# A load of 24 KB to each of 16 partitions, put in the middle of a max-pooling kernel as 15 rows and one row

## The chip, the cores and the metric

One core of one Trainium2 chip. The metric is the device time of one execution in microseconds (us). The kernel before takes 335.85 us (median of 3 runs, 335.66 to 336.07). The profiled span is about 1.8 us shorter than the time of the same run.

## The reference

A one-dimensional max pooling. `x` is 32 x 256 x 4096 in float32; each output is the maximum of 16 consecutive inputs:

```python
def reference(x, output_size):            # output_size = 256, length = 4096
    for i in range(output_size):
        start = int(i * length / output_size)
        end = int((i + 1) * length / output_size)
        result[:, :, i] = np.max(x[:, :, start:end], axis=-1)
```

So 134.2 MB are read, 8.4 MB are written, and each input is used once. There are 2,097,152 windows of 16 elements (64 bytes of input, 4 bytes of output).

## The kernel before

The windows are taken as one long row and dealt to 128 partitions in two groups. Input comes through a ring of three slots. Each slot takes 760 windows per partition (48,640 bytes), VectorE reduces the slot into a result tile, and the results are stored at the end. SyncE issues all DMAs in the order of the program.

```python
    SLOTS = 3
    CHUNK = 760
    GROUPS = [10 * CHUNK, total - 10 * CHUNK]     # windows per partition: 7600, 8784
    ring = pool.tile([P, SLOTS, CHUNK * W], fp32, tag="ring", name="ring")
    # ... (result tiles and DRAM views cut)
    for g, n in enumerate(GROUPS):
        # ... (views of the group cut)
        for a in range(0, n, CHUNK):
            b = min(a + CHUNK, n)
            slot = ring[:, n_loads % SLOTS, 0 : (b - a) * W]
            n_loads += 1
            nc.sync.dma_start(out=slot, in_=xg[:, a * W : b * W])
            nc.vector.reduce_max(out=outs[g][:, a:b],
                in_=slot.rearrange("p (n w) -> p n w", w=W), axis=mybir.AxisListType.X)
        # ... (list of stores cut: group 0; group 1 up to column 7600; the rest)
    for dst, src in stores:
        nc.sync.dma_start(out=dst, in_=src)
```

That makes 22 loads, 21 of them full and the last of 424 windows, and 3 stores.

## Time and profile before

| | before |
|---|---|
| time | 335.85 us |
| DMA queue, share of 16 engines' span | 99.1% |
| VectorE busy | 276.3 us of 334.0 |
| one full load lands every | 14.38 us |
| one full reduction takes | 12.82 us |

From the page of the profile of the kernel before: the span, the busy time of VectorE (DVE), the DMA queue with its packets, megabytes and share of 16 engines' time, the chain of work that ended last, and the group of reductions (busy us, mean ns; then the idle time ahead of them and what ended it).

```profile
span 334.0 us, 111 instructions
...
DVE 276.3 (83%) x22; POOL 0.2 (0%) x4
...
q1 hardware_dynamic: 3600, 142.61, 99.1%
...
DMA 68%; DVE 27%; DVEq 2%; SPq 0%; issue 0%
...
L59 DVE TENSOR_REDUCE out<-ring 128x760 f32<-128x12160 f32 (+1 forms) x22 | 276.3, 12565 | 49.2 <-DMA ring<-in_x_dram 49.2
...
```

The DMA engines have no free time. VectorE waits 49.2 us in all, always for a load. That the chain gives VectorE 27% does not make it a limit: a reduction frees the slot that a later load needs, but that load then stands in a queue that is not empty.

The timeline of the kernel before, at the landings of loads 8 to 11 (loads are counted from 0; start us, length us, engine, line, operation, and in brackets how long the engine was idle and what it waited for):

```profile
...
133.06 12.82 DVE L59 TENSOR_REDUCE out<-ring 128x760 f32<-128x12160 f32 x1 [1.56 <-DMA ring<-in_x_dram]
147.43 12.82 DVE L59 TENSOR_REDUCE out<-ring 128x760 f32<-128x12160 f32 x1 [1.56 <-DMA ring<-in_x_dram]
161.81 12.82 DVE L59 TENSOR_REDUCE out<-ring 128x760 f32<-128x12160 f32 x1 [1.56 <-DMA ring<-in_x_dram]
176.20 12.82 DVE L59 TENSOR_REDUCE out<-ring 128x760 f32<-128x12160 f32 x1 [1.57 <-DMA ring<-in_x_dram]
...
```

Each reduction begins 14.38 us after the one before it, at the moment when its load has landed, after 1.56 us of idling. These starts are therefore the landing times of the loads. From the table of DMA issues (count, KB each, median us from issue to landing), of before:

```profile
...
ring<-in_x_dram SPq DMA_DIRECT2D x21, 6080.0 KB, 30.3
out_dram<-out SPq DMA_DIRECT2D x2, 3800.0 KB, 30.1
...
```

30.3 us is two periods: a load is issued while the load ahead of it still has all of its 14.4 us to go and the one ahead of that its last 1.5 us. The DMA engines thus hold about 16 us of work whenever a new load is issued.

And from the table of stretches of before (columns: from:to, length, busy us and count of VectorE and GpSimd, TensorE clock, mean share of the DMA engines, GB/s):

```profile
...
133.00:147.40 14.40, 12.82 (x1) 0.00 (x0) 1.00 1.00 432
147.40:161.80 14.40, 12.82 (x1) 0.00 (x0) 1.00 1.00 432
...
```

### The profile page before, as it was taken

The page shows a single profiled execution, that of the slowest core. Times are in us where ns is not written, and L with a number is a line of the kernel's source. Part 1 is how long each engine was busy: PE and PEld are TensorE (multiplying, and loading weights), DVE is VectorE, ACT ScalarE, POOL GpSimd, SP SyncE. Part 2 cuts the span into 40 slices and gives each one's busy share as a digit, 9 for nine tenths or more (in the row PEclk, how much of TensorE's full clock was granted, in tenths as well). Part 3 has the DMA queues.
Part 4 walks back from the last instruction along what each step waited for, and adds up shares of the span by engine and source line. Part 5 has one row for each costly group of instructions (what it writes and reads, how often), then busy time and mean ns, then how long its engine had stood idle before and what let it go on. Part 6 is the DMA issues. An engine that isn't in the chain of part 4 may idle for free.

```text
span 334.0 us, 111 instructions
## 1 busy us (share of the span) xinstructions
DVE 276.3 (83%) x22; POOL 0.2 (0%) x4
## 2 busy tenths in 40 slices
DVE  0088989889898988989898898988989898898990
POOL 0000000000000000000000000000000000000000
DMA  9999899999999999999998999999999999989997
GB/s 361 390 460 454 384 466 437 402 466 437 402 460 425 419 454 408 443 454 396 454 454 384 466 437 402 466 419 419 460 414 431 454 408 443 454 384 440 443 419 306
DMA packets 3600, 142.61 MB, mean 427 GB/s; under 512 B 400, under 2 KB 400, under 8 KB 528
## 3 DMA queue, kind: packets, MB, share of 16 engines
q1 hardware_dynamic: 3600, 142.61, 99.1%
HBM read 134.22 MB, written 8.39 MB: 427 GB/s over the span
## 4 chain that ended last, share of the span: by engine, by line
DMA 68%; DVE 27%; DVEq 2%; SPq 0%; issue 0%
DMA ring<-in_x_dram 68%; DVE out L59 27%; DVEq L102 2%; SPq L58 0%
## 5 line engine op out<-in xcount | busy, mean ns | idle before, releaser
L59 DVE TENSOR_REDUCE out<-ring 128x760 f32<-128x12160 f32 (+1 forms) x22 | 276.3, 12565 | 49.2 <-DMA ring<-in_x_dram 49.2
L88 POOL MEMSET const-bfloat16-1.0<- 128x1 bf16 x1 | 0.1, 101 | 0.0
L88 POOL MEMSET const-uint8-127<- 128x1 uint8 x1 | 0.1, 101 | 0.0
L88 POOL MEMSET const-float32-0.0<- 128x1 f32 x1 | 0.1, 98 | 0.2 <-issue 0.2
L88 POOL MEMSET const-float32-1.0<- 128x1 f32 x1 | 0.1, 98 | 0.0
## 6 DMA issues: line engine op xcount, KB each, us to landing
ring<-in_x_dram SPq DMA_DIRECT2D x21, 6080.0 KB, 30.3
out_dram<-out SPq DMA_DIRECT2D x2, 3800.0 KB, 30.1
ring<-in_x_dram SPq DMA_DIRECT2D x1, 3392.0 KB, 23.9
out_dram<-out SPq DMA_DIRECT2D x1, 592.0 KB, 7.6
```

What stands on the lines that cost most here:

```text
L59: nc.vector.reduce_max(out=outs[g][:, a:b], in_=slot.rearrange("p (n w) -> p n w", w=W), axis=mybir.AxisListType.X,)
L88: nc = _bacc.Bacc("TRN2", target_bir_lowering=False, num_devices=1)
L102: with _tile.TileContext(nc) as tc:
```

## The change

One load more is placed after the eleventh load. It takes 384 windows (24,576 bytes) to each of partitions 0 to 15, 393 KB in all, and passes through the ring like any other load. It is issued as two DMAs. The intention was that the one for 15 rows runs on 15 of the 16 DMA engines, and that all 16 share the last row, which is written as 16 pieces. One DMA engine would then carry about 23 KB less than the others (24,576 less 1,536 bytes): an attempt at levelling the engines. The last full-width load shrinks from 424 to 376 windows, so all bytes are still moved exactly once.

```diff
-    total = B * C * O // P
+    total = B * C * O
+    SIDE_P, SIDE, SIDE_AT = 16, 384, 11
+    rest = (total - SIDE_P * SIDE) // P
+    GROUPS = [10 * CHUNK, rest - 10 * CHUNK]
 ... (helpers cut: group(), next_slot(), pooled(), load() do what the loop did)
+    xs, os_ = group(SIDE_P, SIDE)
+    side_out = pool.tile([SIDE_P, SIDE], fp32, tag="side", name="side")
+    def load_side():
+        slot = next_slot(SIDE_P, SIDE)
+        last = SIDE_P - 1
+        nc.sync.dma_start(out=slot[0:last], in_=xs[0:last])
+        nc.sync.dma_start(
+            out=slot[last:SIDE_P].rearrange("p (k n) -> p k n", k=16),
+            in_=xs[last:SIDE_P].rearrange("p (k n) -> p k n", k=16),
+        )
+        pooled(side_out, slot)
 ...
         for a in range(0, n, CHUNK):
+            if n_loads == SIDE_AT:
+                load_side()
+            load(o, xg, a, min(a + CHUNK, n))
 ...
+    stores.insert(1, (os_, side_out))
```

More of the change, by code (lines that the diff above doesn't have):

```diff
@@ L28 @@
     W = L // O
-    total = B * C * O // P
+    total = B * C * O
     SLOTS = 3
     CHUNK = 760
-    GROUPS = [10 * CHUNK, total - 10 * CHUNK]
+    SIDE_P, SIDE, SIDE_AT = 16, 384, 11
+    rest = (total - SIDE_P * SIDE) // P
+    GROUPS = [10 * CHUNK, rest - 10 * CHUNK]
     CUT = 10 * CHUNK
-    assert sum(GROUPS) == total and B * C * O % P == 0
     pool = ctx.enter_context(tc.tile_pool(name="pool", bufs=1))
     ring = pool.tile([P, SLOTS, CHUNK * W], fp32, tag="ring", name="ring")
-    outs = [
-        pool.tile([P, n], fp32, tag=f"out{i}", name=f"out{i}")
-        for i, n in enumerate(GROUPS)
-    ]
@@ L44, with group, next_slot @@
     xw = x.flatten_outer_dims().rearrange("r (o w) -> (r o) w", w=W)
     ow = out.flatten_outer_dims().rearrange("r o -> (r o)")
+    taken = 0
+    def group(parts, n):
+        nonlocal taken
+        span = slice(taken, taken + parts * n)
+        taken += parts * n
+        return (
+            xw[span].rearrange("(p n) w -> p (n w)", p=parts),
+            ow[span].rearrange("(p n) -> p n", p=parts),
+        )
+    n_loads = 0
+    def next_slot(parts, n):
+        nonlocal n_loads
+        slot = ring[0:parts, n_loads % SLOTS, 0 : n * W]
+        n_loads += 1
+        return slot
@@ new lines, in pooled, with load @@
+    def pooled(dst, src):
+        nc.vector.reduce_max(
+            out=dst,
+            in_=src.rearrange("p (n w) -> p n w", w=W),
+            axis=mybir.AxisListType.X,
+        )
+    def load(dst, src, a, b):
+        slot = next_slot(P, b - a)
+        nc.sync.dma_start(out=slot, in_=src[:, a * W : b * W])
+        pooled(dst[:, a:b], slot)
+    xs, os_ = group(SIDE_P, SIDE)
[7 more added lines that the diff above has]
+            in_=xs[last:SIDE_P].rearrange("p (k n) -> p k n", k=16),
+        )
+        pooled(side_out, slot)
@@ L47 @@
     stores = []
-    n_loads = 0
-    first = 0
     for g, n in enumerate(GROUPS):
-        xg = xw[first : first + P * n].rearrange("(p n) w -> p (n w)", p=P)
-        og = ow[first : first + P * n].rearrange("(p n) -> p n", p=P)
-        first += P * n
+        xg, og = group(P, n)
+        o = pool.tile([P, n], fp32, tag=f"out{g}", name=f"out{g}")
         for a in range(0, n, CHUNK):
-            b = min(a + CHUNK, n)
-            slot = ring[:, n_loads % SLOTS, 0 : (b - a) * W]
-            n_loads += 1
-            nc.sync.dma_start(out=slot, in_=xg[:, a * W : b * W])
-            nc.vector.reduce_max(
-                out=outs[g][:, a:b],
-                in_=slot.rearrange("p (n w) -> p n w", w=W),
-                axis=mybir.AxisListType.X,
-            )
-        if g < len(GROUPS) - 1:
-            stores.append((og, outs[g]))
-        else:
-            for a, b in ((0, CUT), (CUT, n)):
-                stores.append((og[:, a:b], outs[g][:, a:b]))
+            if n_loads == SIDE_AT:
+                load_side()
+            load(o, xg, a, min(a + CHUNK, n))
@@ L70 @@
+        for a, b in ((0, CUT), (CUT, n)):
+            if a < b:
+                stores.append((og[:, a:b], o[:, a:b]))
+    assert taken == total
+    stores.insert(1, (os_, side_out))
     for dst, src in stores:
```

## The prediction

> **What bounds the kernel now.** The DMA engines: the queue table gives 99.1% of 16 engines' span. VectorE is busy 276.3 of 334.0 us. In the timeline a full load (128 x 12160) lands every 14.38 us and its reduction takes 12.82 us, so VectorE waits 1.56 us per load. The chain of waits names VectorE (27%) only because a reduction frees a load's slot; that load then still queues behind a whole other one (median 30.3 us from issue to landing, two periods). What matters is bytes per DMA engine, gaps between packets, and which engine finishes last.
>
> In the trace each load has 16 completion arrivals, always spread by 0.92 to 0.96 us: two engines trail (the last 0.13 us behind the second, 0.43 us behind the third). The spread is there at the first load and does not grow: a start offset, not a slow engine.
>
> **What the change does.** Total bytes are the same. The last load shrinks from 6784 to 6016 columns; the 393 KB move into the side load. The order of issues shows one 15x6144 and one 1x6144 DMA after eleven loads, a 16x384 reduction, and one more store.
> [...]
> A 48,640-byte packet takes 1.793 us, 27.1 GB/s per engine.[...] Levelling both laggards could give at most 0.43 us.
>
> **The new hazard.** The side load takes a ring slot for under 1 us of DMA, so the load after it is issued only 1.55 us before the load ahead of the side load lands. The queue then holds about 2.5 us of work, against 16 us normally. At the start, first packets appear 1.0 to 1.4 us after issue (one engine 2.4), and data flows at full rate 1.6 to 2.6 us after it. That nearly fits: I expect one bubble of 0 to 0.4 us[...].
> The side reduction, 6144 elements per partition, costs about 6.5 us of VectorE (from 12.82 us for 12160 and 7.21 for 6784). VectorE falls about 4 us behind and regains 1.56 us per load; the ring's slack hides it. The last reduction is 0.8 us shorter, but the stores queue behind DMA, so no gain.
>
> **Predicted: 336.05 us, from 335.5 to 336.7.** Faster by over 2%: 0.005; within 2%: 0.985; slower by over 2%: 0.01.
>
> **What shows each step.** Queue share still about 99%; full loads 14.38 us apart except one interval of about 15.5 us; VectorE busy about 282 us with a 16-partition reduction near 6.5 us; two or three reductions after it start without waiting; gaps between an engine's packets only just after the side load; the spread of arrivals changed after it.
>
> **What would make it wrong.** The 15-row or one-row DMA on few engines (up to +1 us); [...]a larger bubble (+1 to +3 us); trailing engines really slowed by something the lighter engine relieves (-0.4 us); a different chip's DMA rate.

Where the text shows a cut, passages are taken out that say how the two DMAs are dealt to the DMA engines, which no run had shown, and with them the terms of the sum and two remarks that hang on them. The sum came to about +0.2 us: 0.06 us for the 1.5 KB more assumed on each of 15 engines (at 27.1 GB/s), and three more DMAs at about 0.04 us each, an estimate from the trace of before (14.38 us less 8 packets of 1.793). With 335.85 us before the change that gives 336.05. That the last engine would be spared 23 KB (about 0.8 us) was not expected to shorten the time.

## The result, and the profile after

| | before | after |
|---|---|---|
| time, median (range) | 335.86 us (335.66 to 336.07, 6 runs) | 340.04 us (339.33 to 340.85, 6 runs) |
| span of the profiled run | 334.0 us | 338.5 us |
| DMA queue, share | 99.1% | 98.7% |
| VectorE busy | 276.3 us | 281.9 us |

The ratio is 1.0124 (95% interval 1.0109 to 1.0139): the change makes the kernel 4.2 us slower. Ratios and intervals here and below are from runs of the same rounds, so not quite the ratio of the medians quoted. The loss is within the 2% band, but well above the predicted range.

The page of the changed kernel, the same lines:

```profile
span 338.5 us, 117 instructions
...
DVE 281.9 (83%) x23; POOL 0.2 (0%) x4
...
q1 hardware_dynamic: 3664, 142.61, 98.7%
...
DMA 63%; DVE 30%; issue 3%; DVEq 2%; SPq 0%
...
L67 DVE TENSOR_REDUCE out<-ring 128x760 f32<-128x12160 f32 (+1 forms) x22 | 275.5, 12528 | 48.1 <-DMA ring<-in_x_dram 48.1
L67 DVE TENSOR_REDUCE side<-ring 16x384 f32<-16x6144 f32 x1 | 6.5, 6529 | 0.0
...
```

The DMA share hardly moved, and this is the trap. A packet counts as busy from its start to its end, however slowly it gets on: here packets of 24,576 bytes took up to 3.23 us, where a full load's pace gives 0.91 (below), and all of it is in the share. What the engines moved shows the loss. The table of stretches of the changed kernel:

```profile
...
132.90:147.26 14.36, 12.82 (x1) 0.00 (x0) 1.00 1.00 434
147.26:163.27 16.01, 12.82 (x1) 0.00 (x0) 1.00 1.06 388
163.27:182.00 18.73, 18.71 (x2) 0.00 (x0) 1.00 0.94 393
...
```

The stretch in which load 10 lands is 16.01 us instead of 14.40. The DMA share is there 1.06, over 1 because a packet counts whole in the stretch in which it starts, and the packets that start last in it run long; and yet the rate falls from 434 to 388 GB/s. The timeline of the changed kernel shows where:

```profile
...
132.91 12.82 DVE L67 TENSOR_REDUCE out<-ring 128x760 f32<-128x12160 f32 x1 [1.57 <-DMA ring<-in_x_dram]
145.75 0.40 SPq L84 DMA_DIRECT2D ring<-in_x_dram  x1
146.21 0.23 SPq L85 DMA_DIRECT2D ring<-in_x_dram  x1
147.28 12.82 DVE L67 TENSOR_REDUCE out<-ring 128x760 f32<-128x12160 f32 x1 [1.56 <-DMA ring<-in_x_dram]
160.13 35.51 SPq L75 DMA_DIRECT2D ring<-in_x_dram  x4
163.29 12.82 DVE L67 TENSOR_REDUCE out<-ring 128x760 f32<-128x12160 f32 x1 [3.19 <-DMA ring<-in_x_dram]
176.03 6.53 DVE L67 TENSOR_REDUCE side<-ring 16x384 f32<-16x6144 f32 x1
182.49 12.80 DVE L67 TENSOR_REDUCE out<-ring 128x760 f32<-128x12160 f32 x1
195.73 12.82 DVE L67 TENSOR_REDUCE out<-ring 128x760 f32<-128x12160 f32 x1 [0.45 <-DMA ring<-in_x_dram]
```

The side load is issued at 145.75 and 146.21. Load 10, which was issued ahead of it, lands at 163.27, 16.01 us after load 9; VectorE idles 3.19 us instead of 1.56. The side reduction takes 6.53 us although it has 16 partitions: its time goes by the elements per partition (6144; the run own_step_8 below reduces 128 partitions of 6144 in 6.54 us). The next full load lands at 181.33 by the trace's completion records; VectorE is behind at that point and takes it up at 182.49. From the landing of load 9 to that of the next full load but one, 147.26 to 181.33, are 34.07 us, and 28.76 in the kernel before. Of the difference of 5.3 us the last, smaller load gives 0.9 back. What is left, 4.4 us, is nearly all of the 4.5 us by which the spans differ: the loss lies at this one place.

In the same trace, the packets around the side load look like this (times worked out from the packets' records):

```
                                          packets   us each: shortest, median, longest
full loads, undisturbed (48,640 bytes)                1.79    1.80    1.81
side load (24,576 bytes)                     16       1.95    2.64    3.23
first packets of the load behind it          16       1.80    3.13    4.59
```

At the pace of a full load's packets (48,640 bytes, most often in 1.796 us) a packet of 24,576 bytes should take 0.91 us. It took nearly three times as long, and the first packets behind it were slow too. After that nearly every packet takes 1.80 us again. The records do not name the engines, but on each engine one packet starts where the one before it ends, so they can be linked into 16 chains. One chain has two of the side packets, one after the other (160.78 to 163.63 and 163.63 to 166.18), and one has none. The engine with two is then late for good. The 16 completion arrivals of a full load spread over 0.70 us ahead of the side load and over 2.33 us in every load after it, the last of them 0.85 us after the second to last.

The table of DMA issues of the changed kernel:

```profile
...
ring<-in_x_dram SPq DMA_DIRECT2D x21, 6080.0 KB, 30.3
...
ring<-in_x_dram SPq DMA_DIRECT2D x1, 360.0 KB, 20.3
ring<-in_x_dram SPq DMA_DIRECT2D x1, 24.0 KB
...
```

The row of 24 KB has no time to landing, where all others have one. Its completion records explain that: one arrival recorded when it was issued (146.61) and one at 167.27. The DMA of 15 rows has one at its issue (146.28) and 15 later ones, from 164.12 to 166.02. A full load has 16. So the row ran on one DMA engine, as one packet of 24,576 bytes: the trace has 16 packets of that size and none of 1,536 bytes in the loads. The trace's record of the instruction itself (L85) already has one element of 24,576 bytes as its destination, not 16 of 1,536: the pieces were already joined in the instruction.

### The profile page after: what moved, and what is told of

Its sections match the earlier page's. It is cut to its first block, busy times and chain, and to the rows that moved or that the text cites. A ratio compares the mean times of both kernels' runs of the same rounds, so it can differ in the third digit from the quotient of the medians.

```text
span 338.5 us, 117 instructions
## 1 busy us (share of the span) xinstructions
DVE 281.9 (83%) x23; POOL 0.2 (0%) x4
## 3 DMA queue, kind: packets, MB, share of 16 engines
q1 hardware_dynamic: 3664, 142.61, 98.7%
## 4 chain that ended last, share of the span: by engine, by line
DMA 63%; DVE 30%; issue 3%; DVEq 2%; SPq 0%
DMA ring<-in_x_dram 63%; DVE out L67 28%; DVE side L67 2%; DVEq L137 2%; SPq L75 0%
## 5 line engine op out<-in xcount | busy, mean ns | idle before, releaser
L67 DVE TENSOR_REDUCE side<-ring 16x384 f32<-16x6144 f32 x1 | 6.5, 6529 | 0.0
```

The lines of the kernel that those rows point to most:

```text
L67: nc.vector.reduce_max(out=dst, in_=src.rearrange("p (n w) -> p n w", w=W), axis=mybir.AxisListType.X,)
```

## The experiments

Three suspects came out of this:

- **P, place.** All 393 KB go to 16 neighbouring partitions, where a full load goes to 128. The slow side packets (a median of 2.64 us instead of 0.91) would then come from where they land.
- **S, split.** The sixteenth row went whole to one DMA engine that already had a row (the chain with two side packets).
- **L, late issue.** The side load occupies a ring slot for little DMA time, so the load behind it is issued with about 2.5 us of work left in the queue instead of 16 (an estimate: 1.56 us of the load ahead, VectorE's wait in the timeline of before, and 0.9 of the side load at a full load's pace).

A fourth, **H**, was that one contiguous piece of 393 KB is slow to read from HBM.

Twelve kernels ran, all correct, on three different chips; before's medians were 335.83, 335.79 and 335.75 us. "Price" below is the difference of the medians of a kernel and of before. P's figures in some expectations, and M's below, rested on an assumption about the receiving side that no run here shows; they are cut, with the cut marked. What is left of P there is its direction: the time depends on the partitions that the rows go to.

### one_dma: all 16 rows in one DMA

```diff
-        nc.sync.dma_start(out=slot[0:last], in_=xs[0:last])
-        nc.sync.dma_start(out=slot[last:SIDE_P]..., in_=xs[last:SIDE_P]...)   # k = 16 pieces
+        nc.sync.dma_start(out=slot, in_=xs)
```

> All 16 side rows go in one DMA into partitions 0 to 15; everything else as in the changed kernel (340.04 us). Theory P[...]: the side rows all land in 16 neighbouring partitions[...]; on top of it the sixteenth row went whole to one engine, which had a row already, and that engine is last by about 0.9 us. P expects 339.1 us (0.9 less), the spread of a later load's arrivals down from 2.3 to about 1.4 us. Rival S (split): the uneven split is the whole loss: 336.1 us. Rival L (late issue): the load behind the side load is issued too late, the split hardly matters: 339.5 to 340. Rival H (HBM): reading one contiguous 393 KB piece is slow: 339.1 as P.

Measured: 339.21 us, ratio 1.0098 [1.0083, 1.0113], price 3.4 us. The spread of the arrivals after the side load fell to 1.10 us. The split explains 0.8 us of the loss and not more: S alone is refuted.

### row_on_16: the sixteenth row really on all engines

```diff
-        nc.sync.dma_start(out=slot[last:SIDE_P].rearrange("p (k n) -> p k n", k=16), in_=...)
+        for h in (0, 192):
+            nc.sync.dma_start(
+                out=slot[last:SIDE_P].rearrange("p (k n) -> p k n", k=16)[:, :, h : h + 192],
+                in_=xs[last:SIDE_P].rearrange("p (k n) -> p k n", k=16)[:, :, h : h + 192])
```

Each of the two DMAs leaves gaps, so its 16 pieces cannot be joined into one run.

> The side load as it was intended: 15 rows in one DMA, and the sixteenth in two DMAs of 16 pieces of 768 bytes with gaps, which can not be joined into one run and so should use all engines. P: 339.2 us, no engine last by 0.9 us; both DMAs of the sixteenth row show 16 completion arrivals instead of one. S: 336.1. L: 339.5 to 340.

Measured: 339.35 us, ratio 1.0101 [1.0084, 1.0118], the same as one_dma within the noise. Its five runs range from 339.13 to 341.02 us, and their mean, 339.75, is only 0.3 us under the changed kernel's, so the gain of this run is not sure by itself. The cost of the split again: own_place less own_one_dma, below, is 0.8 us. Both DMAs of the row show 16 arrivals, and the table of DMA issues of this run now has a time to landing for them:

```profile
...
ring<-in_x_dram SPq DMA_DIRECT2D x1, 360.0 KB, 20.2
ring<-in_x_dram SPq DMA_DIRECT2D x2, 12.0 KB, 19.7
...
```

The trace's records of its two instructions have 16 elements of 768 bytes each. So the pieces of the changed kernel had been joined, and with the split as it was meant the loss would still have been 3.5 us.

### spread_8: partitions 0, 8, ... 120, through the ring

```diff
-        slot = next_slot(SIDE_P, SIDE)
-        nc.sync.dma_start(out=slot, in_=xs)                      # as in one_dma
+        slot = next_slot(P, SIDE)
+        nc.sync.dma_start(out=slot[::8], in_=xs)
+    stores.insert(1, (os_, side_out[::8]))                       # side_out has 128 partitions
```

The ring is made of three tiles here instead of one, so that the strided write is not taken for a conflict with the other slots. The reduction runs over all 128 partitions; rows that were not loaded hold old data and are not stored.

> As one_dma (16 rows in one DMA, same source), but the rows land in partitions 0, 8, 16 ... 120, and the reduction runs over 128 partitions of 6144 elements (same VectorE time; rows not loaded hold old data and are not stored). [...] H and L: no change from one_dma (339.1 and 339.5 to 340).

Measured: 338.18 us, ratio 1.0074 [1.0058, 1.0091]. The side packets took a median of 1.62 us, against 2.97 in one_dma. The time fell by 1.0 us, where H and L had expected no change: the destination matters.

### even_128: the same bytes over 128 partitions, through the ring

```diff
-    SIDE_P, SIDE, SIDE_AT = 16, 384, 11
+    SIDE_P, SIDE, SIDE_AT = 128, 48, 11        # one DMA, as in one_dma
```

> The same 393 KB from the same place, as one extra load over all 128 partitions (3072 bytes each) at the same point, through the same ring slot[...]. VectorE has 0.9 instead of 6.5 us more. P: 336.2 us, within 0.3 of the kernel before. H: 339.1 as one_dma. L: the load behind it is issued just as late, so 338.5 or more.

Measured: 338.02 us, ratio 1.0064 [1.0049, 1.0079], price 2.2 us. P had expected to come within 0.3 us of before. With all 128 partitions as the destination something still costs 2.2 us. The timeline of this run:

```profile
...
145.61 0.33 SPq L83 DMA_DIRECT2D ring<-in_x_dram  x1
...
160.00 32.50 SPq L75 DMA_DIRECT2D ring<-in_x_dram  x4
161.54 12.82 DVE L67 TENSOR_REDUCE out<-ring 128x760 f32<-128x12160 f32 x1 [1.57 <-DMA ring<-in_x_dram]
174.28 0.94 DVE L67 TENSOR_REDUCE side<-ring 128x48 f32<-128x768 f32 x1
179.32 12.82 DVE L67 TENSOR_REDUCE out<-ring 128x760 f32<-128x12160 f32 x1 [4.10 <-DMA ring<-in_x_dram]
...
```

The load behind the side load is issued at 160.00. The side load is over at 162.01 (end of its last packet), and VectorE then idles 4.10 us for the next load. Twelve of the 16 DMA engines begin that load by 162.02, but the first packets of the other four start at 162.25, 162.63, 163.03 and 163.77. The last engine got its work 3.8 us after the issue. In the first load of the kernel before, all but one of the first packets appeared 1.0 to 1.4 us after the issue, and the prediction had reckoned with that. Late issue is a cost of its own.

### own_place: the change as it is, but without taking a ring slot

```diff
-        slot = next_slot(SIDE_P, SIDE)
+        slot = o[0:SIDE_P, rest - 10 * CHUNK - SIDE * W :]
```

The side rows land in columns of the second result tile that are written only later. The side load and all loads behind it are then issued as early as in the kernel before.

> The changed kernel with one thing undone: the side rows do not take a ring slot but land in columns of the second result tile that are written only later, so the loads behind them are issued as early as in the kernel before (16 us ahead instead of about 2). Still 15 rows and one row, still partitions 0 to 15. The extra load over 128 partitions through a ring slot cost 2.2 us, 16 neighbouring partitions 1.2 us more, the split 0.8 more. Theory L+P+S, costs that add: 337.8 us (340.04 less 2.2). Theory M (the costs hide each other: a side load that lasts longer gives the load behind it more time[...] and the late issue shows only in part)[...]. If late issue is nothing: 340.0.

Measured: 340.45 us, ratio 1.0140 [1.0123, 1.0157]. Taking the late issue away gave nothing back. The costs do not add; they hide each other. The likely reason is that as long as the crowded side load blocks the DMA engines, the load behind it has time to be issued: in the changed kernel the side packets end 2.3 to 6.1 us after the issue of that load (160.13; 162.43 to 166.18), in even_128 the last of them 2.0 us after it. M's direction is right. The other two pairs of runs with and without the ring slot show the same grading: the slot costs 2.2 us with 128 partitions (even_128 less own_even_128, prices 2.2 and 0.05), 1.2 us with every eighth partition (spread_8 less own_step_8, prices 2.4 and 1.2), and nothing with partitions 0 to 15 (one_dma 3.4, own_one_dma below 3.8).

### own_one_dma: the destination alone

The edits of own_place and one_dma together.

> As the run with its own place, but the 16 rows in one DMA. [...] If costs add: 337.0 us (335.85 + 1.2). [...]

Measured: 339.62 us, ratio 1.0108 [1.0093, 1.0123], price 3.8 us. Costs that add would have given 337.0 us, and a destination that costs nothing the time of before. In the timeline the load is issued at 131.68, two loads ahead, and load 10 still lands late:

```profile
...
131.68 0.42 SPq L83 DMA_DIRECT2D out<-in_x_dram  x1
...
147.22 12.82 DVE L67 TENSOR_REDUCE out<-ring 128x760 f32<-128x12160 f32 x1 [1.56 <-DMA ring<-in_x_dram]
163.40 12.82 DVE L67 TENSOR_REDUCE out<-ring 128x760 f32<-128x12160 f32 x1 [3.36 <-DMA ring<-in_x_dram]
176.14 6.53 DVE L67 TENSOR_REDUCE side<-out 16x384 f32<-16x6144 f32 x1
...
```

VectorE's wait ahead of the reduction at 163.40 is 3.36 us. Here no late issue and no uneven split is left. Side packets take 1.96 to 3.66 us, and the 16 first packets behind them 2.30 to 4.67 us.

### own_even_128: neither crowded, nor late, nor split

The edits of own_place and even_128 together.

> The extra load over 128 partitions, but in its own place: no ring slot taken[...]. Both theories with a late issue expect 336.0 us, within 0.3 of the kernel before (338.02 with a ring slot); loads still 14.38 us apart plus 0.95 once, spread of arrivals unchanged at the end. If an extra small load in the middle costs by itself, whatever its slot: about 338.

Measured: 335.84 us, ratio 1.0000 [0.9985, 1.0015].

```profile
...
131.66 0.43 SPq L83 DMA_DIRECT2D out<-in_x_dram  x1
...
161.61 12.82 DVE L67 TENSOR_REDUCE out<-ring 128x760 f32<-128x12160 f32 x1 [1.59 <-DMA ring<-in_x_dram]
174.34 0.94 DVE L67 TENSOR_REDUCE side<-out 128x48 f32<-128x768 f32 x1
176.93 12.82 DVE L67 TENSOR_REDUCE out<-ring 128x760 f32<-128x12160 f32 x1 [1.64 <-DMA ring<-in_x_dram]
...
```

Loads land as before, with the side load's own 0.95 us added once (161.59 to 162.54 in the completion records). Every first packet behind it takes 1.81 to 1.82 us. An extra load in the middle costs nothing by itself. It reads the same 393 KB from the same place, though in shorter rows; own_step_8 below keeps the rows of 24 KB too and costs 1.2 us where own_one_dma costs 3.8. So H does not explain the loss.

### even_144: through the ring slot, three times as large

```diff
-    SIDE_P, SIDE, SIDE_AT = 128, 48, 11        # even_128
+    SIDE_P, SIDE, SIDE_AT = 128, 144, 11
```

> The extra load over 128 partitions through the ring slot, three times as large (144 windows, 9216 bytes per partition; the last load is smaller by as much). Nothing else differs. It keeps the DMA engines 2.7 us instead of 0.9, so the load behind it is issued 4.2 us before it is needed instead of 2.4. With 48 windows that load's first packet came to the last engine 3.8 us after issue. Late issue: 336.1 us, the loss gone. If an extra load in a ring slot costs whatever its lead: 338 us or more.

Measured: 335.70 us, ratio 0.9996 [0.9981, 1.0011].

```profile
...
161.49 12.82 DVE L67 TENSOR_REDUCE out<-ring 128x760 f32<-128x12160 f32 x1 [1.56 <-DMA ring<-in_x_dram]
174.23 2.54 DVE L67 TENSOR_REDUCE side<-ring 128x144 f32<-128x2304 f32 x1
178.66 12.82 DVE L67 TENSOR_REDUCE out<-ring 128x760 f32<-128x12160 f32 x1 [1.89 <-DMA ring<-in_x_dram]
...
```

A larger load through the same slot costs nothing, while the smaller one cost 2.2 us. What counts is the lead: the last side packet ends 3.85 us after the issue of the load behind it (159.96 to 163.81), and 2.0 us after it in even_128. VectorE waits 1.89 us ahead of the load behind it, not 4.10.

### own_32, own_64 and own_step_8: is it the place, or the number of rows?

Three runs with one DMA, an early issue and the same 393 KB:

```diff
-    SIDE_P, SIDE, SIDE_AT = 16, 384, 11        # own_one_dma
+    SIDE_P, SIDE, SIDE_AT = 32, 192, 11        # own_32: partitions 0 to 31
+    SIDE_P, SIDE, SIDE_AT = 64, 96, 11         # own_64: partitions 0 to 63
```

own_step_8 keeps 16 rows of 24 KB and writes them to partitions 0, 8, ... 120 (`out=slot[::8]`), in a tile of their own that is a late part of the second result; it has one more store.

> The side rows in their own place and one DMA, as the run that cost 3.8 us with 16 partitions and nothing with 128; now 32 rows of half the length in partitions 0 to 31. [...] Rival N (fewer and longer rows are slow[...]; the price falls by half with each doubling of rows): 337.7.

> The same with 64 rows of a quarter of the length in partitions 0 to 63. [...] N: half of the price of 32 partitions, 336.7 us or less.

> 16 whole rows of 24 KB in one DMA as in the run that cost 3.8 us, same source, same row length, but to partitions 0, 8, 16 ... 120[...]. The landing place is a part of the second result tile that is written later (made a tile of its own, so one more store, and a memset at the start while VectorE idles: about 0.05 us). [...] N, or any reason in the row length or the engines: 339.6, as with partitions 0 to 15.

The reductions around the side load in the timelines of own_64 and of own_step_8:

```profile
...
163.01 12.82 DVE L67 TENSOR_REDUCE out<-ring 128x760 f32<-128x12160 f32 x1 [2.87 <-DMA ring<-in_x_dram]
175.74 1.73 DVE L67 TENSOR_REDUCE side<-out 64x96 f32<-64x1536 f32 x1
...
```

```profile
...
162.79 12.82 DVE L67 TENSOR_REDUCE early<-ring 128x760 f32<-128x12160 f32 x1 [2.68 <-DMA ring<-in_x_dram]
175.53 6.54 DVE L67 TENSOR_REDUCE side<-out 128x384 f32<-128x6144 f32 x1
...
```

VectorE waits 2.87 and 2.68 us for load 10, between the 3.36 of 16 neighbouring partitions and the 1.59 of 128 partitions. In numbers:

| run | rows | time | price | ratio [95%] |
|---|---|---|---|---|
| own_one_dma | 16, partitions 0 to 15 | 339.62 | 3.8 us | 1.0108 [1.0093, 1.0123] |
| own_32 | 32, partitions 0 to 31 | 337.35 | 1.6 us | 1.0045 [1.0028, 1.0061] |
| own_64 | 64, partitions 0 to 63 | 337.34 | 1.6 us | 1.0044 [1.0029, 1.0059] |
| own_step_8 | 16, every eighth partition | 336.94 | 1.2 us | 1.0037 [1.0022, 1.0052] |
| own_even_128 | 128 | 335.84 | 0.05 us | 1.0000 [0.9985, 1.0015] |

32 and 64 neighbouring partitions cost the same, 1.6 us, and 16 long rows cost a third when they are only spread out, 1.2 us instead of 3.8. The number and the length of the rows (N) do not explain that. The first run, at 337.35 us, does not speak against N (337.7), but own_64 (337.34; N: 336.7 or less) and own_step_8 (336.94; N: 339.6) do. So the price in these runs goes by the partitions in which the rows land; what these partitions share, and why 64 cost as much as 32, no run shows. VectorE's longer side reduction is no explanation either: it takes 6.54 us in own_step_8 and 1.73 us in own_64, and own_step_8 is not the slower one.

### own_192: half the bytes to the same 16 partitions

```diff
-    SIDE_P, SIDE, SIDE_AT = 16, 384, 11        # own_one_dma
+    SIDE_P, SIDE, SIDE_AT = 16, 192, 11
```

> 16 rows of half the length (12 KB, 197 KB in all) in one DMA to partitions 0 to 15, own place. P with a price in proportion to the bytes: 1.9 of 3.8 us, 337.7 us. [...]

Measured: 337.33 us, ratio 1.0048 [1.0033, 1.0063], price 1.6 us of 3.8. The price goes with the bytes (half would be 1.9). A price that does not depend on the bytes would have given the 339.62 us of own_one_dma and is refuted. A straight line through 1.6 us for half of the bytes and 3.8 for all leaves nothing for a fixed part.

## Why the prediction was wrong, point by point

- **The step that failed: the sum of +0.2 us for the side load.** It priced the side load at the rate of the sending engines, 27.1 GB/s each (48,640 bytes in 1.793 us), as if the receiving side were free. The engines were spread and the destinations were not. Sent to 16 neighbouring partitions, the same bytes cost 3.8 us by themselves (own_one_dma); sent to 128, nothing (own_even_128); sent to every eighth partition, or to 32 or 64 neighbouring ones, 1.2 to 1.6 us. This is the main term of the loss, and the prediction did not have it. The trace of before could not give it: each of its loads goes to all 128 partitions.
- **The sixteenth row was to be shared by all engines: wrong.** The row arrived as one packet on one DMA engine, with one completion arrival. The loss falls by 0.8 us when the row is joined to the 15 (one_dma: 340.04 to 339.21; own_place to own_one_dma: 340.45 to 339.62), and by 0.7, less surely, when its pieces are kept apart (row_on_16: 339.35). The 15 rows did go as intended: 15 arrivals came late and one at the issue. The prediction listed "the 15-row or one-row DMA on few engines (up to +1 us)" as a danger and put it outside its sum.
- **The lighter engine gave no gain that could be seen.** In the chains of packets the spared engine is the one that was last to finish load 10 (161.68, the next to last 161.47); for that case the prediction expected no gain. It idled 0.41 us, and its first packet of the next load took 3.88 us although it had no side packet: it was held up with the others and finished that packet at 165.97, the others theirs from 166.18 on. The spread of arrivals that the change could have levelled is not fixed anyway: it was 0.94 us in the profiled run of before and 0.70 in that of the changed kernel ahead of the side load, and from 0.5 to 1.3 us in other runs.
- **"One bubble of 0 to 0.4 us": too small as a price, though right as a danger.** In a side load that crowds nothing it costs 2.2 us (even_128), since the last engine's work arrives 3.8 us after the issue and not 1.0 to 2.4. In the changed kernel it is hidden behind the crowded side load: own_place removed it and gained nothing.
- **What held.** VectorE is busy 281.9 us (282 expected) and the side reduction takes 6.53 us (6.5 expected); its delay is absorbed by the ring and the last, shorter reduction gains nothing (own_even_128 has it too and takes the time of before). Full loads away from the side load still come 14.38 us apart. The DMA share stayed at about 99%, which was expected, but it was no evidence of health.

Put together for the changed kernel: about 3.4 us for the crowded side load with its late issue (one_dma) and 0.8 us for the split, 4.2 in all.

What stays open: what in the destination sets the price (3.8 us for partitions 0 to 15, 1.6 for 0 to 31 and for 0 to 63, 1.2 for every eighth). In own_one_dma the side packets together took 2.05 us per engine more than at full pace, and the first packets of the load behind them 1.38 us more. The second part is seen, but no run tells whether it is the same backlog still draining or a slow start of the engines on the next load. The times speak for the backlog: these first packets start from 162.40 to 165.23 but all end between 166.57 and 167.67, soon after the last side packet (165.23), whenever they started. Also open: no run spreads 16 rows of 24 KB in another way than over every eighth partition, so a price of 0 is shown for 128 short rows alone.

## What to carry to other kernels

Count a DMA's destination as well as its engines: in a stream that fills the DMA engines, a small load to a few neighbouring partitions blocks all of them (3.8 us here for 393 KB), so give the same bytes to all 128 partitions (0.05 us here). If a small load takes a slot of a ring, check how much queued work is left when the load behind it is issued; here 2.0 us was too little and 3.9 us enough. And do not take a DMA share near 100% for full speed: look at the GB/s of the stretch, at the packets' times and at the number of completion arrivals of each DMA.
